# RWKV preparation: the inverse of the cumulative decay by a second scan and one Newton step

## The chip, the cores and the metric

The kernel runs on one core of a Trainium2 chip. The metric is device time in microseconds (us) from start to end of the program; the kernel before takes 1405.99 us (median of three runs, 1405.21 to 1406.52). The engines are named as the profile names them: PE is TensorE's matmul side and PEld its weight load, DVE is VectorE, ACT is ScalarE, POOL is GpSimd, SP is the queue from which most DMAs are issued.

## The reference, cut to what matters

One decoder layer for 1024 tokens and width 1024: a mixing part (HGRN2, windowed attention and RWKV-7 side by side), an MLP with a short convolution, a gated embedding, a final norm. The change lies in the RWKV-7 part, whose reference is a recurrence over the tokens with a per-channel decay:

```python
w = -jax.nn.softplus(-(w0 + jnp.tanh(wd) @ w2)) - 0.5
decay = jnp.exp(-jnp.exp(w))
a = jax.nn.sigmoid(a0 + ad @ a2)
...
def step(state, inp):
    r_t, w_t, k_t, v_t, kk_t, a_t = inp
    sa = jnp.einsum('bhvk,bhk->bhv', state, -kk_t)
    state = (state * w_t[:, :, None, :] + sa[..., None] * (kk_t * a_t)[:, :, None, :]
             + v_t[..., None] * k_t[:, :, None, :])
    return state, jnp.einsum('bhvk,bhk->bhv', state, r_t)
```

The decay of a token equals exp(-e^-0.5 * s), where s is the sigmoid of the decay's low-rank projection. The kernel does not walk through the tokens one by one. It works in chunks of 64 tokens, and for each chunk needs the running product of the decays from the chunk's start (gamma) and its inverse 1/gamma, for each channel and token.

## The kernel before, in words

Everything is held with channels on the 128 partitions and tokens along the free dimension, 1024 of them, in two halves of 512. A projection is a product of a 1024 x 128 block of weights with the normed input; both are split into a high and a low part, and three matmuls (lines 137, 139 and 141) stand in for one. A block's 48 matmuls write a `dp` tile, of which there are two in PSUM. Before that its weights come by DMA (`wraw`, line 105), ACT makes the high part (`whi`, line 114), and POOL or DVE the low part (`wlo`, line 116), in turn.

The RWKV part runs twice, for channel pair p = 0 and p = 1 (each 128 channels, two heads). In each, `rwkv_prep` makes the operands: k by a projection and a mix with the previous token (`mix_in`), the sums of squares of its key (`kks`), the decay `w` and the gate `a` (sigmoids on ACT, lines 568 and 571, from two small matmuls each), then exp (line 572), the scan that gives `gam` (line 581), the reciprocals that give `ig` (line 584, two halves), `ai = a * ig` (586), r by another projection (its `mix_in` scales the `dp` tile in line 320 and reads it a last time in line 502), `kkn`, `bhat` (602), and `ar` (609). A scan over a whole row would run across chunks. So the first column of each chunk is copied into `dz`, which is zero elsewhere, and set to zero in `w`: the step state = w * state + dz then starts anew at each chunk.

`bhat` and `ar` go into 32 small matmuls, the scores (`sc`, line 654 in `rwkv_scores`). They are masked (656), written to DRAM and read back in another layout (`scz`, `At`, lines 664 and 670). `rwkv_inverse` then inverts 32 x 32 blocks on DVE: 31 pairs of a multiply and an add (lines 678 and 680). The result goes through DRAM once more (`Tz`, `Tc`, lines 685 and 690) and `rwkv_join` multiplies with it (`py`, line 790), with which `rwkv_main` begins.

PE has other work in the meantime: `project_rest`, a generator that projects blocks for the later parts. It is called `fill`, and the prep and the inverse draw steps from it.

What sets the order of the work: the code is recorded once, and a scheduler then fixes the order of the instructions of each engine by its own estimates of their durations. At run time each engine and each DMA queue works strictly in that order, and an instruction that waits holds up all that stands behind it on its engine. The scheduler also gives out buffers: the tiles with tag `tr` share eight.

Of the kernel before, what the change touches and what calls it, by code (L numbers as in the profile page):

```python
# [13 lines left out]
AF = mybir.ActivationFunctionType  # L14
ALU = mybir.AluOpType
# [5 lines left out]
HT = 512  # L21
# [4 lines left out]
EXP_M05 = math.exp(-0.5)  # L26
# [4 lines left out]
PC_W0, PC_A0, PC_KK, PC_KA, PC_RK, PC_LNW, PC_LNB = 48, 50, 52, 54, 56, 58, 60  # L31
# [58 lines left out]
class Trunk:  # L90
# [446 lines left out]
    def rwkv_prep(self, p, tp, lt, d, fill):  # L537

        nc, par = self.nc, self.par

        def tr(name):
            return tp.tile([P, T], F32, tag="tr", name=self.nm(name), bufs=8)

        def col(c):
            return par[:, c + p:c + p + 1]

        k = self.mix_in(2 + 3 * p, 2 + p, "k", tr)
        if p == 0:
            self.load_masks(tp)
            self.ps0.close()  # L550
            self.mxp = self.psm.enter_context(self.pool("mx", bufs=4, space=PSUM))
        mxp = self.mxp

        sq = tr("kksq")
        nc.scalar.activation(sq, k, AF.Square, scale=col(PC_KK))
        pss = mxp.tile([P, 16], F32, tag="mx", name=self.nm("kks"))
        for tb in range(8):
            nc.tensor.matmul(pss[:, 2 * tb:2 * tb + 2], sq[:, tb * P:(tb + 1) * P], self.bone2, start=True, stop=True)
        r1 = self.spool.tile([P, 16], F32, tag="kr1", name=self.nm("kr1"), bufs=1)
        nc.vector.tensor_scalar(r1, pss, 1e-24, None, ALU.max)  # L560
        r2 = self.spool.tile([P, 16], F32, tag="kr2", name=self.nm("kr2"), bufs=1)
        nc.gpsimd.tensor_tensor(r2, r1, self.mhalf, ALU.pow)
        w, a = tr("w"), tr("a")
        for hf in (0, 1):
            sl = slice(hf * HT, (hf + 1) * HT)
            ps = mxp.tile([P, HT], F32, tag="mx", name=self.nm("lo"))
            nc.tensor.matmul(ps, par[0:64, PC_LORA + p * P:PC_LORA + (p + 1) * P], lt[0:64, sl], start=True, stop=True)
            nc.scalar.activation(w[:, sl], ps, AF.Sigmoid, bias=col(PC_W0))
            ps = mxp.tile([P, HT], F32, tag="mx", name=self.nm("lo"))
            nc.tensor.matmul(ps, par[64:128, PC_LORA + p * P:PC_LORA + (p + 1) * P], lt[64:128, sl], start=True, stop=True)  # L570
            nc.scalar.activation(a[:, sl], ps, AF.Sigmoid, bias=col(PC_A0))
        nc.scalar.activation(w, w, AF.Exp, scale=-EXP_M05)

        dz = tr("dz")
        w3 = w.rearrange("p (c i) -> p c i", i=64)
        dz3 = dz.rearrange("p (c i) -> p c i", i=64)
        nc.gpsimd.memset(dz, 0.0)
        nc.vector.tensor_copy(dz3[:, :, 0:1], w3[:, :, 0:1])
        nc.vector.memset(w3[:, :, 0:1], 0.0)
        gam = tr("gam")  # L580
        nc.vector.tensor_tensor_scan(gam, w, dz, 0.0, ALU.mult, ALU.add)
        ig = tr("ig")
        for hf in (0, 1):
            nc.vector.reciprocal(ig[:, hf * HT:(hf + 1) * HT], gam[:, hf * HT:(hf + 1) * HT])  # L584
        ai = tr("ai")
        nc.vector.tensor_tensor(ai, a, ig, ALU.mult)
        r = self.mix_in(3 + 3 * p, 0 + p, "r", tr)

        kkn = tr("kkn")
        for hf in (0, 1):  # L590
            sl = slice(hf * HT, (hf + 1) * HT)
            pb = mxp.tile([P, HT], F32, tag="mx", name=self.nm("kkb"))
            self.spread2(pb, r2[:, 8 * hf:8 * hf + 8], 4)
            nc.vector.scalar_tensor_tensor(kkn[:, sl], k[:, sl], self.nkk[:, p:p + 1], pb, ALU.mult, ALU.mult)
        ar = self.slots.tile([P, 2, 16, 64], F32, tag="rk_ar", name=self.nm("ar"), bufs=1)

        def c3(t):
            return t.rearrange("p (c i) -> p c i", i=64)

        g3, kk3 = c3(gam), c3(kkn)  # L600
        be, kh = self.slot("bhat"), self.slot("khat")
        nc.vector.scalar_tensor_tensor(be, ai, -1.0, kkn, ALU.mult, ALU.mult)
        def pairs(t, odd, turn=False):
            t = t.rearrange("p (a b) i -> p a b i", b=4)[:, :, 2 * odd:2 * odd + 2]
            return t[:, :, ::-1] if odd and turn else t

        for odd in (0, 1):
            a4, k4, g4 = pairs(ar[:, 0], odd, True), pairs(kk3, odd), pairs(g3, odd)
            nc.vector.tensor_tensor(a4[:, :, :, 1:], k4[:, :, :, 1:], g4[:, :, :, :63], ALU.mult)
            nc.scalar.copy(a4[:, :, :, 0:1], k4[:, :, :, 0:1])  # L610
        d.update(ar=ar, be=be, kh=kh)
        for _ in range(6 if p else 8):
            next(fill)
        self.rwkv_scores(p, tp, d)
        if p:
            d["v"] = self.mix_in(4 + 3 * p, 4 + p, "v")

        t = tr("ka")
        nc.vector.tensor_scalar(t, a, -1.0, col(PC_KA), ALU.add, ALU.mult)
        nc.vector.scalar_tensor_tensor(k, t, 1.0, k, ALU.add, ALU.mult)  # L620
        for odd in (0, 1):
            nc.vector.tensor_tensor(pairs(ar[:, 1], odd, True), pairs(c3(r), odd), pairs(g3, odd), ALU.mult)
        nc.gpsimd.tensor_tensor(kh, k, ig, ALU.mult)
        gC = self.spool.tile([P, 16], F32, tag="gC", name=self.nm("gC"), bufs=1)
        self.gap = nc.vector.tensor_copy(gC.unsqueeze(2), g3[:, :, 63:64]).ins
        bv = self.slot("bv")
        nc.vector.scalar_tensor_tensor(bv, r, col(PC_RK), k, ALU.mult, ALU.mult)
        d.update(bv=bv, gC=gC)
# [1231 lines left out]
```

## Time and profile before

| | |
|---|---|
| median of three runs | 1405.99 us |
| profiled execution | 1404.77 us |
| its span, first to last instruction | 1403.0 us |
| PE, DVE, ACT, POOL busy | 98%, 76%, 44%, 28% of the span |
| prep of p = 0, and of p = 1 | about 47 to 80 us, and 214 to 242 us |
| two reciprocals of one prep, back to back | 6.55 us (p = 0), 6.57 us (p = 1) |
| one scan | 2.29 us |

A row of the timeline gives the start in us from the span's start, the duration in us, engine, line, operation, the tiles as out<-in, and in brackets the idle time before it and what ended it. A row of the windows gives the stretch, its length, then for PE, PEld, DVE, ACT and POOL the busy time and (in brackets) the number of instructions, and at its end the granted PE clock, the DMA share and GB/s. A row of the waits gives who waited for whom, the total in us, how often, and the longest.

### The profile page before, as it was taken

Reading aid. Unit: us, or ns where it says so; the run is one execution under the profiler, and the core shown is the slowest. Engines: PE = TensorE matmul, PEld = TensorE weight load, DVE = VectorE, ACT = ScalarE, POOL = GpSimd, SP = SyncE. Lnnn points to the kernel's source line nnn. Section 1 sums busy time; section 2 is a strip of 40 time slices with the busy share of each in tenths; the row PEclk is TensorE's granted clock in tenths of the full one; section 3 lists DMA queues with packets and bytes.
Section 4 is the critical chain, followed back from the end, with each engine's and each line's share of the span. In section 5 each row is a group of like instructions: output and inputs, shape, how many; then the busy total and the mean of one; then the engine's idle time right before and its main releaser. Section 6 shows DMA issues by size and latency. Waiting matters only on the chain.

```text
span 1403.0 us, 22344 instructions
## 1 busy us (share of the span) xinstructions
PE 1375.7 (98%) x8644; PEld 1116.5 (80%) x8644; DVE 1063.7 (76%) x1613; ACT 611.8 (44%) x1049; POOL 395.5 (28%) x287
## 2 busy tenths in 40 slices
PE   9999999999999999999999999999999999999997
PEld 6878777877878768788788888888888888888886
DVE  7696456835667796468889888888988799777685
ACT  7522323133255584255544343444344444455542
POOL 5411012101222242221345454545453000002342
PEclk9999999999999999999999999999999999999998
DMA  6123111321622212653232332332324963441443
GB/s 224 61 83 104 64 61 47 100 73 62 225 83 99 91 61 71 253 180 125 94 127 98 113 103 90 102 105 98 114 98 166 351 217 106 127 143 45 136 138 140
DMA packets 80122, 167.61 MB, mean 119 GB/s; under 512 B 19984, under 2 KB 22288, under 8 KB 80016
## 3 DMA queue, kind: packets, MB, share of 16 engines
q1 hardware_dynamic: 66784, 147.05, 31.3%
q10 hardware_dynamic: 12224, 15.47, 3.2%
q0 software_dynamic: 1008, 3.67, 0.7%
q8 instruction: 68, 1.11, 0.3%
q14 instruction: 38, 0.31, 0.1%
HBM read 119.76 MB, written 46.40 MB: 118 GB/s over the span
## 4 chain that ended last, share of the span: by engine, by line
PE 78%; DVE 8%; issue 8%; ACT 3%; POOL 3%; DMA 1%; SPq 0%; POOLq 0%; ACTq 0%; DVEq 0%
PE bg L1338 17%; PE bv L1338 13%; PE bv L1639 7%; PE bg L1639 7%; PE dp L137 7%; PE dp L139 7%; PE dp L141 7%; PE swq L1169 1%; DVE ig L584 1%; PE hsc L1015 1%; PE zp L137 1%; DVE xl L409 1%; PE zp L141 1%; PE zp L139 1%; PE swo L1209 1%
## 5 line engine op out<-in xcount | busy, mean ns | idle before, releaser
L137 PE MATMUL dp<-xh,whi 128*128 128x512 f32 x544 | 186.9, 406 | 1.2 <-DVE r L502 0.7
L139 PE MATMUL dp<-xl,whi 128*128 128x512 f32 x544 | 180.5, 394 | 0.6 <-DVE xl L409 0.5
L141 PE MATMUL dp<-xh,wlo 128*128 128x512 f32 x544 | 179.7, 392 | 0.0
L116 POOL TENSOR_TENSOR wlo<-wraw,whi 128x512 fp32r<-128x512 f32 x60 | 84.5, 1410 | 264.9 <-ACT whi L114 226.8
L116 POOL TENSOR_TENSOR wlo<-raw,whi 128x512 fp32r<-128x512 f32 x84 | 135.0, 1626 | 75.9 <-ACT whi L114 75.9
L114 ACT CAST whi<-wraw 128x512 fp32r<-128x512 f32 x120 | 72.9, 618 | 158.0 <-PE dp L139 103.0
L1338 PE MATMUL bg<-t,whi 128*128 128x512 f32 x352 | 133.4, 389 | 0.0
L139 PEld LDWEIGHTS dp<-xl,whi 128*128 128x128 f32 x544 | 102.3, 188 | 24.6 <-DVE xl L409 2.5
L141 PEld LDWEIGHTS dp<-xh,wlo 128*128 128x128 f32 x544 | 102.2, 188 | 23.8 <-issue 2.0
L137 PEld LDWEIGHTS dp<-xh,whi 128*128 128x128 f32 x544 | 98.8, 189 | 26.0 <-issue 3.9
L116 POOL TENSOR_TENSOR wlo<-s,whi 128x512 fp32r<-128x512 f32 x44 | 64.5, 1466 | 168.6 <-ACT whi L114 168.6
L1639 PE MATMUL bg<-t,whi 128*128 128x512 f32 x308 | 95.2, 390 | 0.0
L1639 PE MATMUL bv<-t,whi 128*128 128x512 f32 x308 | 94.8, 389 | 0.0
L114 ACT CAST whi<-raw 128x512 fp32r<-128x512 f32 x88 | 52.7, 620 | 93.7 <-issue 48.5
L114 ACT CAST whi<-s 128x512 fp32r<-128x512 f32 x66 | 38.9, 620 | 120.2 <-PE bg L1338 112.8
L1338 PEld LDWEIGHTS bg<-t,whi 128*128 128x128 f32 x352 | 66.1, 188 | 13.7
L190 POOL TENSOR_TENSOR rst<-rst,mhalf 128x4 f32<-128x4 f32 (+1 forms) x9 | 10.2, 1134 | 234.0 <-DVE rst L186 218.0
L1635 ACT CAST t<-t 128x512 fp32r<-128x512 f32 x77 | 47.8, 622 | 45.8 <-PE bv L1639 32.7
L1338 PE MATMUL bg<-t,wlo 128*128 128x512 f32 x176 | 67.5, 389 | 0.0
L1639 PEld LDWEIGHTS bv<-t,whi 128*128 128x128 f32 x308 | 57.8, 188 | 12.0
L1639 PEld LDWEIGHTS bg<-t,whi 128*128 128x128 f32 x308 | 57.8, 188 | 11.9
L116 DVE TENSOR_TENSOR wlo<-wraw,whi 128x512 fp32r<-128x512 f32 x60 | 48.2, 807 | 20.7 <-ACT whi L114 18.5
(417 smaller groups left out, 3423.6 us busy)
## 6 DMA issues: line engine op xcount, KB each, us to landing
raw<-in_ffn_up_dram SPq DMA_DIRECT2D x44, 512.0 KB, 3.5
wraw<-in_w_in_dram SPq DMA_DIRECT2D x28, 512.0 KB, 3.4
z<-zst SPq DMA_DIRECT2D x18, 512.0 KB, 2.9
gb<-ct SPq DMA_DIRECT2D x33, 256.0 KB, 2.3
t<-gb SPq DMA_DIRECT2D x33, 256.0 KB, 2.7
t<-gt SPq DMA_DIRECT2D x33, 256.0 KB, 2.7
zl<-z SPq DMA_DIRECT2D x16, 512.0 KB, 4.4
wraw<-in_ple_gate_dram SPq DMA_DIRECT2D x16, 512.0 KB, 3.4
```

The costliest lines, as they stand in the source:

```text
L114: self.cast = nc.scalar.copy(hi, src).ins
L116: eng.tensor_tensor(lo, src, hi.bitcast(F32), ALU.subtract)
L137: nc.tensor.matmul(ps[hf], wh, xh[hf], start=first, stop=False)
L139: nc.tensor.matmul(ps[hf], wh, xl[hf], start=False, stop=False)
L141: self.step = nc.tensor.matmul(ps[hf], wl, xh[hf], start=False, stop=last).ins
L409: nc.vector.scalar_tensor_tensor(lo, x, g[:, k:k + 1], hi.bitcast(F32), ALU.mult, ALU.subtract)
L584: nc.vector.reciprocal(ig[:, hf * HT:(hf + 1) * HT], gam[:, hf * HT:(hf + 1) * HT])
L1015: nc.tensor.matmul(sc[g:g + 64, c, :], ks[:, c * P + g:c * P + g + 64], x, start=True, stop=True)
L1169: m = nc.tensor.matmul(pq[h][:, b:b + w], d["q"][hs, qb * P:nk], d["k"][hs, b:b + w], start=True, stop=True)
L1338: nc.tensor.matmul(ps, w[part == 2][:, s], X[k][part == 1], start=start and k == part == 0, stop=k == 3 and part == 2, skip_group_check=no ...
L1635: nc.scalar.copy(xh, x)
L1639: nc.tensor.matmul(ps[m], wt[part == 2][:, m * P:(m + 1) * P], (xh, xl)[part == 1], start=k == part == 0, stop=k == NK - 1 and part == 2)
```

## The change: what it does, and the diff

ACT computes a second exponential, exp(+e^-0.5 * s), the inverse of a token's decay, into the tile `gam`, ahead of the exponential of the decay itself. For p = 1 the last sigmoid of `a` is fixed behind both exponentials. DVE then scans twice: the running product of the inverses goes into `ig`, then that of the decays into `gam`. Two fused steps take the place of the reciprocals, and do one Newton step on `ig`: w = -gam * ig, then ig = (w + 2) * ig. So per prep there are one activation, one scan, two fused steps of 128 x 1024, one copy and one memset of 128 x 16 more, and two reciprocals of 128 x 512 less. No DMA and no matmul is added or removed.

```diff
-            nc.scalar.activation(a[:, sl], ps, AF.Sigmoid, bias=col(PC_A0))
-        nc.scalar.activation(w, w, AF.Exp, scale=-EXP_M05)
+            if not (p and hf):
+                nc.scalar.activation(a[:, sl], ps, AF.Sigmoid, bias=col(PC_A0))
+        gam = tr("gam")
+        nc.scalar.activation(gam, w, AF.Exp, scale=EXP_M05)
+        m = nc.scalar.activation(w, w, AF.Exp, scale=-EXP_M05)
+        if p:
+            with self.tc.issue_after(m.ins):
+                nc.scalar.activation(a[:, sl], ps, AF.Sigmoid, bias=col(PC_A0))
 
         dz = tr("dz")
-        w3 = w.rearrange("p (c i) -> p c i", i=64)
         dz3 = dz.rearrange("p (c i) -> p c i", i=64)
         nc.gpsimd.memset(dz, 0.0)
-        nc.vector.tensor_copy(dz3[:, :, 0:1], w3[:, :, 0:1])
-        nc.vector.memset(w3[:, :, 0:1], 0.0)
-        gam = tr("gam")
-        nc.vector.tensor_tensor_scan(gam, w, dz, 0.0, ALU.mult, ALU.add)
         ig = tr("ig")
-        for hf in (0, 1):
-            nc.vector.reciprocal(ig[:, hf * HT:(hf + 1) * HT], gam[:, hf * HT:(hf + 1) * HT])
+        for src, dst in ((gam, ig), (w, gam)):
+            s3 = src.rearrange("p (c i) -> p c i", i=64)
+            nc.vector.tensor_copy(dz3[:, :, 0:1], s3[:, :, 0:1])
+            nc.vector.memset(s3[:, :, 0:1], 0.0)
+            nc.vector.tensor_tensor_scan(dst, src, dz, 0.0, ALU.mult, ALU.add)
+        nc.vector.scalar_tensor_tensor(w, gam, -1.0, ig, ALU.mult, ALU.mult)
+        nc.vector.scalar_tensor_tensor(ig, w, 2.0, ig, ALU.add, ALU.mult)
         ai = tr("ai")
```

In the changed file the new scan is line 588, the fused steps are 589 and 590, and what stands behind them has a line number 6 higher than before (the scores are line 660).

The change also moves instructions that it does not name, because the scheduler orders them anew. On PE, in p = 0, before (`dp_619` is one block of `fill`, `dp_827` the next):

```order
L141 MATMUL dp_619<-xh_119,wlo_617 128x512
L141 MATMUL dp_619<-xh_103,wlo_617 128x512
L137 MATMUL dp_827<-xh_105,whi_646 128x512
L137 MATMUL dp_827<-xh_89,whi_646 128x512
L139 MATMUL dp_827<-xl_106,whi_646 128x512
L139 MATMUL dp_827<-xl_90,whi_646 128x512
L141 MATMUL dp_827<-xh_105,wlo_648 128x512
L141 MATMUL dp_827<-xh_89,wlo_648 128x512
L137 MATMUL dp_827<-xh_107,whi_646 128x512
L137 MATMUL dp_827<-xh_91,whi_646 128x512
L139 MATMUL dp_827<-xl_108,whi_646 128x512
L654 MATMUL sc_679<-ar_601,bhat_602 64x64
```

and of the change (the same two blocks are `dp_623` and `dp_831`):

```order
L141 MATMUL dp_623<-xh_119,wlo_621 128x512
L141 MATMUL dp_623<-xh_103,wlo_621 128x512
L660 MATMUL sc_683<-ar_605,bhat_606 64x64
L660 MATMUL sc_684<-ar_605,bhat_606 64x64
L660 MATMUL sc_683<-ar_605,bhat_606 64x64
```

The scores now stand straight behind the first block; the nine matmuls of the next block that stood ahead of them come after all 32 of them.

On PE, in p = 1, before (`dp_2263` is a block of `fill`, `dp_2361` the projection of v):

```order
L141 MATMUL dp_2263<-xh_99,wlo_2261 128x512
L137 MATMUL dp_2361<-xh_105,whi_2353 128x512
L137 MATMUL dp_2361<-xh_89,whi_2353 128x512
L139 MATMUL dp_2361<-xl_106,whi_2353 128x512
L139 MATMUL dp_2361<-xl_90,whi_2353 128x512
L141 MATMUL dp_2361<-xh_105,wlo_2355 128x512
L141 MATMUL dp_2361<-xh_89,wlo_2355 128x512
L137 MATMUL dp_2361<-xh_107,whi_2353 128x512
L137 MATMUL dp_2361<-xh_91,whi_2353 128x512
L139 MATMUL dp_2361<-xl_108,whi_2353 128x512
L139 MATMUL dp_2361<-xl_92,whi_2353 128x512
L654 MATMUL sc_2311<-ar_2245,bhat_2246 64x64
```

and of the change (`dp_2263` is `dp_2271` there):

```order
L141 MATMUL dp_2271<-xh_99,wlo_2269 128x512
L660 MATMUL sc_2319<-ar_2253,bhat_2254 64x64
L660 MATMUL sc_2320<-ar_2253,bhat_2254 64x64
L660 MATMUL sc_2319<-ar_2253,bhat_2254 64x64
L660 MATMUL sc_2320<-ar_2253,bhat_2254 64x64
```

Here ten matmuls of the projection of v, among them the one that had to wait for a free `dp` tile, are moved behind the scores.

On POOL, in p = 1, before (`khat` is line 623, `Tb` the memsets ahead of the inverse):

```order
L116 TENSOR_TENSOR wlo_2359<-wraw_2351,whi_2357 128x512
L116 TENSOR_TENSOR wlo_2564<-wraw_2556,whi_2562 128x512
L672 MEMSET Tb_2431 64x1024
L673 MEMSET Tb_2431 64x32
L623 TENSOR_TENSOR khat_2247<-k_2117,ig_2156 128x1024
L116 TENSOR_TENSOR wlo_2629<-wraw_2625,whi_2627 128x512
```

and of the change:

```order
L116 TENSOR_TENSOR wlo_2367<-wraw_2359,whi_2365 128x512
L678 MEMSET Tb_2439 64x1024
L679 MEMSET Tb_2439 64x32
L116 TENSOR_TENSOR wlo_2572<-wraw_2564,whi_2570 128x512
L116 TENSOR_TENSOR wlo_2637<-wraw_2633,whi_2635 128x512
L629 TENSOR_TENSOR khat_2255<-k_2121,ig_2158 128x1024
```

`khat` now comes behind a second `wlo`. On DVE the new steps stand in the order of the code, with r's scaling (line 320) ahead of the second scan's copy in p = 0 and between the two fused steps in p = 1; the small copy `gC` comes ahead of `ai` in both. On SP the weight load that stood on one side of the reads of `At` stands on the other: in p = 0 it is now ahead of them, in p = 1 behind them.

## The prediction, made before the changed kernel ran

> **What bounds the kernel now.** I read first the page's shares, then the windows around the two places that the change touches, then PE's waits there.
>
> ```profile
> span 1403.0 us, 22344 instructions
> PE 1375.7 (98%) x8644; PEld 1116.5 (80%) x8644; DVE 1063.7 (76%) x1613; ACT 611.8 (44%) x1049; POOL 395.5 (28%) x287
> ```
> ```profile
> 47.00:80.00 33.00, 32.03 (x230) 25.54 (x229) 26.30 (x29) 16.09 (x21) 9.55 (x5) 1.00 0.10 33
> 80.00:132.00 52.00, 52.00 (x227) 42.36 (x226) 41.83 (x84) 11.20 (x16) 8.77 (x8) 1.00 0.37 107
> 214.00:242.00 28.00, 26.61 (x204) 20.57 (x203) 20.72 (x23) 9.93 (x14) 5.07 (x3) 1.00 0.06 20
> 242.00:290.00 48.00, 48.00 (x209) 38.73 (x207) 36.66 (x79) 5.88 (x9) 9.79 (x8) 1.00 0.35 108
> ```
> PE is the bound: in the preps (first and third row) it is busy 32.03 of 33 and 26.61 of 28 us, and behind each it has no hole at all (52.00 of 52.00, 48.00 of 48.00). Its clock is 1.00 in all four. So a faster DVE is worth only what PE waits for it in the preps:
>
> ```profile
> PE sc L654 <- DVE ar L609: 1.4, 2, 0.8
> PE dp L137 <- DVE r L502: 0.7, 1, 0.7
> ```
> That is 2.1 us in the whole program (the scores of both preps, and once a `dp` tile that r's last read frees). It is the ceiling on what this change can win. What it can lose is not bounded by it, since PE's order changes as well.
>
> **DVE's part: what the new steps cost.** For p = 0:
>
> ```profile
> 60.44 0.19 DVE L578 COPY dz<-w 128x16 f32<-128x16 f32 x1 [5.18 <-ACT w L572]
> 60.81 2.29 DVE L581 TENSOR_TENSOR_SCAN gam<-w,dz 128x1024 f32<-128x1024 f32 x1
> 63.02 1.21 DVE L320 TENSOR_TENSOR dp<-dp,rstd 128x1024 f32<-128x1024 f32 x1
> 64.14 6.55 DVE L584 RECIPROCAL ig<-gam 128x512 f32<-128x512 f32 x2
> 70.73 1.23 DVE L586 TENSOR_TENSOR ai<-a,ig 128x1024 f32<-128x1024 f32 x1
> 75.04 1.22 DVE L602 SCALAR_TENSOR_TENSOR bhat<-ai,kkn 128x1024 f32<-128x1024 f32 x1
> ```
> From the start of the reciprocals to `ai`: 70.73 - 64.14 = 6.59 us. In their place stand a copy and memset (start to start of the scan 60.81 - 60.44 = 0.37), a scan (2.29), and two fused steps. These have two SBUF operands of 128 x 1024, as `bhat` has, so 1.22 each. Sum 0.37 + 2.29 + 2.44 = 5.10, with some 0.15 for `gC`'s place and for steps that each need the one before: 5.25. DVE gains 6.59 - 5.25 = 1.3 us. ACT's new exponential lies under the first scan: that scan needs the first exponential alone, and starts when it did.
>
> For p = 1:
>
> ```profile
> 222.37 2.29 DVE L581 TENSOR_TENSOR_SCAN gam<-w,dz 128x1024 f32<-128x1024 f32 x1
> 224.70 6.57 DVE L584 RECIPROCAL ig<-gam 128x512 f32<-128x512 f32 x2
> 231.18 1.21 DVE L320 TENSOR_TENSOR dp<-dp,rstd 128x1024 f32<-128x1024 f32 x1
> 232.29 1.21 DVE L586 TENSOR_TENSOR ai<-a,ig 128x1024 f32<-128x1024 f32 x1
> ```
> The reciprocals take 231.18 - 224.70 = 6.48 on the path, the new steps 5.2: again 1.3. The chain from `ai` to `ar` is the same in both versions, so the scores are ready 1.3 us earlier, if nothing else holds the new steps up.
>
> **What holds them up: POOL.**
>
> ```profile
> 61.46 2.74 POOL L116 TENSOR_TENSOR wlo<-wraw,whi 128x512 fp32r<-128x512 f32 x1 [2.54 <-ACT whi L114]
> 69.01 1.30 POOL L116 TENSOR_TENSOR wlo<-wraw,whi 128x512 fp32r<-128x512 f32 x1 [4.81 <-ACT whi L114]
> 89.56 1.30 POOL L116 TENSOR_TENSOR wlo<-wraw,whi 128x512 fp32r<-128x512 f32 x1 [7.39 <-ACT whi L114]
> ```
> ```profile
> 89.61 1.29 DVE L678 TENSOR_TENSOR Tt<-At,Tb 64x31 f32<-64x31 f32 x1
> 253.70 0.17 DVE L678 TENSOR_TENSOR Tt<-At,Tb 64x31 f32<-64x31 f32 x1
> ```
> A multiply that takes 0.17 us took 1.29 when POOL's `wlo` began just before it (89.56): it stood still for 1.1 us, until POOL was done (90.86). The other way round, the `wlo` of 61.46 met the running scan, and took 2.74: it ended 1.1 us after the scan's end (63.10). But the `wlo` of 69.01 ran its usual 1.30 beside the reciprocals, and those took no longer. So a reciprocal and a `wlo` pass each other, a two-operand step and a `wlo` exclude each other, and the one that asked first goes first. The change replaces the former kind by the latter. In p = 0 the second fused step runs from about 64.14 + 0.37 + 2.29 + 1.22 = 68.0 to 69.3, so POOL's `wlo`, ready at 69.01, waits for it and then goes ahead of `ai`: `ai` loses about 1.1. For p = 1:
>
> ```profile
> 220.84 1.06 ACT L572 ACTIVATE w<-w 128x1024 f32<-128x1024 f32 x1
> 224.02 0.62 ACT L114 CAST whi<-wraw 128x512 fp32r<-128x512 f32 x1
> ```
> The cast that stood at 224.02 comes 1.06 later, behind the new exponential, and ends at 225.7; its `wlo` then meets the second scan (about 225.0 to 227.3), waits for its end, and goes ahead of the first fused step: 1.1 lost again. So of DVE's gain g = 1.3 there is left 0.2 in each prep. The bounds of g are 0.2 (hit) and 1.3 (missed); I take 0.2, since the hit in p = 1 has a window of 2.3 us, and that in p = 0 one of about 1.2.
>
> The Trainium skill, SBUF — State Buffer, section "SBUF: two separate sides", states this as a lock: DVE with two SBUF inputs and a GpSimd operation that reads SBUF share one pair of ports, the first has it for its whole instruction, the other is blocked. The rows above agree with it, and by it the sum is the one with g = 0.2; without it, that with g = 1.3.
>
> **PE's part: the scores are moved forward.** PE's rows in p = 0:
>
> ```profile
> 73.73 0.39 PE L141 MATMUL dp<-xh,wlo 128*128 128x512 f32 x1
> 75.78 0.39 PE L139 MATMUL dp<-xl,whi 128*128 128x512 f32 x1
> 77.00 1.52 PE L654 MATMUL sc<-ar,bhat 64*64 64x64 f32 x64 [0.83 <-DVE ar L609]
> ```
> Before, PE ended its last matmul ahead of the scores at 75.78 + 0.39 = 76.17, and stood for 0.83 until 77.00. Now the nine matmuls from 73.96 on stand behind the scores. PE comes to them at 73.73 + 0.39 = 74.12 and stands until 77.00 - g, so 2.88 - g. The nine are done later, but nothing fills the hole. The loss is 2.88 - g - 0.83 = 2.05 - g: 1.85 us with g = 0.2, 0.75 with 1.3. And in p = 1:
>
> ```profile
> 234.10 0.61 PE L141 MATMUL dp<-xh,wlo 128*128 128x512 f32 x2
> 235.41 0.72 PE L137 MATMUL dp<-xh,whi 128*128 128x512 f32 x2 [0.70 <-DVE r L502]
> 237.37 0.63 PE L139 MATMUL dp<-xl,whi 128*128 128x512 f32 x2
> 238.55 1.52 PE L654 MATMUL sc<-ar,bhat 64*64 64x64 f32 x64 [0.56 <-DVE ar L609]
> ```
> Before: a wait of 0.70 for the tile and 0.56 for `ar`, together 1.26. Now PE is free at 234.10 + 0.61 = 234.71 and stands until 238.55 - g, so 3.84 - g; the tile is free by then. Loss 2.58 - g: 2.38 with g = 0.2, 1.28 with 1.3. Since PE has no hole behind, every later matmul moves by as much.
>
> **POOL's `khat`, and the inverse.** Behind the scores of p = 1, `khat` moves from a stretch in which DVE waits to one where it works:
>
> ```profile
> 246.06 2.39 POOL L623 TENSOR_TENSOR khat<-k,ig 128x1024 f32<-128x1024 f32 x1
> 251.91 1.27 POOL L116 TENSOR_TENSOR wlo<-wraw,whi 128x512 fp32r<-128x512 f32 x1 [3.46 <-ACT whi L114]
> ```
> ```profile
> 250.09 1.28 DVE L627 SCALAR_TENSOR_TENSOR bv<-r,par,k 128x1024 f32<-128x1024 f32 x1
> ```
> ```profile
> 290.32 0.24 PE L790 MATMUL py<-Tc,sc 32*32 32x32 f32 x2
> 290.96 1.19 PE L790 MATMUL py<-Tc,sc 32*32 32x32 f32 x62
> PEld py L790 <- DMA Tc<-Tz: 0.8, 2, 0.5
> ```
> It follows the second `wlo`, the one that stood at 251.91 and whose cast now comes ahead of v's step on ACT, so it falls on `bv` (250.09) or on the first multiplies of the inverse, all with two operands. It costs that chain between 0 (it falls beside steps that read PSUM) and 2.4 (its whole length); I take 1.0, near the 1.1 of a usual block. The chain ends in `Tc`, and there is no slack: `py` started as its weights came (the last row), PE stood between its two pieces, and so 1.0 goes to PE. In p = 0 `khat` keeps its place. There a `wlo` of DVE (0.7) moves into the inverse, and the weight load goes ahead of `At` on SP; the reads of `Tc` are issued long before `py` there:
>
> ```profile
> 125.55 2.18 SPq L690 DMA_DIRECT2D Tc<-Tz  x4
> ```
> until 127.73, and PE has work until about 132.8. I cost these at nothing; cover gone, they would cost about 0.7. ACT's later casts (by 1.06) feed blocks that PE reaches many us later: nothing.
>
> **Sum.** 1.85 + 2.38 + 1.0 = 5.2 us. The profiled execution took 1404.77 (span 1403.0), so 1410.0; the median of the runs is 1.2 above it, 1405.99, so 1411.2.
>
> **Rivals.** *No collision:* POOL misses the new steps, g = 1.3, and `khat` costs nothing: 0.75 + 1.28 = 2.0, time 1408.0. For it: POOL's starts depend on tenths of a us. With one or two of the three hits, 3.1 to 4.2 are lost (1409.1 to 1410.2). *Not slower:* the fused steps are cheaper than `bhat`'s row, and the scheduler was right to move the scores. The point where this decides is g = 2.05 in p = 0 and 2.58 in p = 1; each fused step would need (6.59 - 2.05 - 2.81) / 2 = 0.87, or (6.48 - 2.58 - 2.81) / 2 = 0.55 us, where 2.81 is the rest of the 5.25. At that point the time is 1406.0, and at the ceiling of 2.1 us won 1403.9. Against it: 1.22 in two places for this shape. *More collisions:* `khat` costs its full 2.4, and p = 0's inverse comes late by 0.7: 1.85 + 2.38 + 2.4 + 0.7 = 7.3, time 1413.3.
>
> **How the numbers follow.** Forecast (all three costs) 0.45; one or two of the three 0.13; no collision 0.14; not slower 0.10; more collisions 0.12; something else 0.06. A measurement of this kernel can tell 0.2%, 2.8 us, from no change. Slower: 0.45 + 0.13 + 0.12 = 0.70. Within 0.2%: 0.14 and nearly all of "not slower", 0.23. Faster: 0.07, all but from what I don't see, since even the ceiling of 2.1 us does not reach it. The range leaves out "not slower" and a little on top: 1406.5 to 1413.8.
>
> **What will show it.** Right: PE's wait at the scores is 2.5 to 2.8 us in p = 0 and 3.5 to 3.8 in p = 1 and the one for r's tile is gone; `ai` (p = 0) and the first fused step (p = 1) last about 2.3 us beside a `wlo`; the fused steps otherwise last 1.22; `py` of p = 1 waits 1 us longer. Wrong: waits at the scores under 1 us, which would mean cheaper steps, or later stretches in which PE wins back what it lost.

## The result, and the profile after

The kernel after the change takes 1414.65 us (median of six runs, 1412.75 to 1415.97), the kernel before 1405.7 us beside it. The ratio is 1.0065, with a 95% interval of 1.0054 to 1.0076: slower by some 9 us, where 5.2 were forecast. The direction was right, and the size falls just outside the range (1413.8).

The page of the profiled execution, which took 1412.75 us:

```profile
span 1411.0 us, 22350 instructions
PE 1377.6 (98%) x8644; PEld 1119.1 (79%) x8644; DVE 1063.7 (75%) x1619; ACT 613.4 (43%) x1051; POOL 397.2 (28%) x287
```

The span is 8.0 us longer than before (1403.0). PE's busy time grew by 1.9 us, though it runs the same 8644 matmuls; the other 6.1 us are waits. The windows around the two preps, as shown of the kernel before:

```profile
47.00:80.00 33.00, 30.29 (x222) 24.10 (x221) 25.92 (x30) 17.86 (x23) 8.80 (x5) 1.00 0.09 33
80.00:132.00 52.00, 52.00 (x227) 42.36 (x226) 40.66 (x85) 9.77 (x15) 8.50 (x7) 1.00 0.37 103
214.00:242.00 28.00, 24.33 (x165) 19.05 (x167) 19.28 (x22) 12.00 (x16) 7.84 (x5) 0.96 0.11 38
242.00:290.00 48.00, 47.88 (x237) 38.60 (x230) 36.00 (x73) 5.98 (x9) 9.75 (x6) 0.95 0.28 94
```

In the preps (first and third row) PE is busy 1.74 and 2.28 us less than before. What is new stands near the end of the rows, in the column of the granted clock: 0.96 and 0.95 around 242 us, where it was 1.00. PE's waits in whole:

```profile
PE sc L660 <- DVE ar L615: 6.3, 3, 3.6
PE py L796 <- DMA Tc<-Tz: 0.6, 1, 0.6
```

The wait at the scores is 6.3 us (2.46 and 0.25 for p = 0, 3.56 for p = 1), where there were 1.4 before; the wait of 0.7 us for r's `dp` tile is gone; at `py` of p = 1 PE stands for 0.57 us between its two pieces, where it stood for 0.40 before (290.96 - 290.32 - 0.24). PE's rows at the scores, first p = 0, then p = 1:

```profile
77.33 0.34 PE L660 MATMUL sc<-ar,bhat 64*64 64x64 f32 x8 [2.46 <-DVE ar L615]
77.92 1.04 PE L660 MATMUL sc<-ar,bhat 64*64 64x64 f32 x56 [0.25 <-DVE ar L615]
...
240.72 2.36 PE L660 MATMUL sc<-ar,bhat 64*64 64x64 f32 x64 [3.56 <-DVE ar L615]
243.02 1.22 PE L137 MATMUL dp<-xh,whi 128*128 128x512 f32 x2
...
246.59 0.71 PE L139 MATMUL dp<-xl,whi 128*128 128x512 f32 x2
247.14 0.62 PE L141 MATMUL dp<-xh,wlo 128*128 128x512 f32 x2
247.60 0.62 PE L137 MATMUL dp<-xh,whi 128*128 128x512 f32 x2
```

Behind the hole of p = 1 the same work takes longer. The 64 small matmuls of the scores last 2.36 us instead of 1.52. The eight large matmuls from 243.02 on need 3.57 us (246.59 - 243.02), where eight at the pace of the last two rows (two in 247.60 - 247.14 = 0.46) need 1.84. Together PE loses 0.84 + 1.73 = 2.6 us there. The windows of 2 us show why:

```profile
238.00:240.00 2.00, 0.00 (x0) 0.00 (x0) 2.00 (x4) 0.31 (x2) 0.00 (x0) 0.98 0.00 0
240.00:242.00 2.00, 1.17 (x33) 1.04 (x37) 2.00 (x3) 0.00 (x0) 1.09 (x2) 0.50 0.00 0
242.00:244.00 2.00, 2.00 (x45) 1.73 (x38) 2.00 (x6) 0.00 (x0) 0.00 (x0) 0.50 0.03 8
244.00:246.00 2.00, 2.00 (x6) 1.57 (x5) 1.49 (x3) 0.00 (x0) 0.00 (x0) 0.50 0.44 178
246.00:248.00 2.00, 2.00 (x8) 1.60 (x8) 0.00 (x0) 0.00 (x0) 0.00 (x0) 0.81 0.21 85
```

The clock is granted at half from about 239.9 to 246.8 us, that is from near the end of a hole of 3.56 us in which PE did nothing. Behind the hole of 2.46 us in p = 0 it stayed at 1.00 in this execution (second row of the first windows).

So the 8.0 us are, by rows: 1.88 more of waiting at the scores of p = 0 (2.46 + 0.25 - 0.83), 2.30 at those of p = 1 (3.56 - 1.26), and 2.6 of half clock; 1.2 are left. Of these, 0.7 us stand ahead of the first prep already, where DVE's first new step starts at 61.18 us, its counterpart before at 60.44. The rest falls far behind the preps: the same matmuls run 7.4 us later than before at 500 us and 8.1 us later at 527 us, on either side of the wait for `vt`.

DVE's rows, p = 0 and p = 1, and then the two rows of POOL that fall on them:

```profile
67.57 1.23 DVE L589 SCALAR_TENSOR_TENSOR w<-gam,ig 128x1024 f32<-128x1024 f32 x1
...
70.09 2.20 DVE L592 TENSOR_TENSOR ai<-a,ig 128x1024 f32<-128x1024 f32 x1
...
229.95 2.13 DVE L589 SCALAR_TENSOR_TENSOR w<-gam,ig 128x1024 f32<-128x1024 f32 x1
233.14 1.21 DVE L590 SCALAR_TENSOR_TENSOR ig<-w,ig 128x1024 f32<-128x1024 f32 x1
```
```profile
69.76 1.45 POOL L116 TENSOR_TENSOR wlo<-wraw,whi 128x512 fp32r<-128x512 f32 x1 [4.83 <-ACT whi L114]
...
228.05 2.95 POOL L116 TENSOR_TENSOR wlo<-wraw,whi 128x512 fp32r<-128x512 f32 x1 [4.83 <-ACT whi L114]
```

A fused step takes 1.21 to 1.23 us, as forecast. `ai` takes 2.20 behind the `wlo` of 69.76, and the first fused step of p = 1 takes 2.13 behind the `wlo` of 228.05, which had waited for the end of the scan: both collisions, in the places named.

### The profile page after: what moved, and what is told of

It reads as the page before. It is cut to its first block, busy times and chain, and to the rows that moved or that the text cites. A ratio compares the mean times of both kernels' runs of the same rounds, so it can differ in the third digit from the quotient of the medians.

```text
span 1411.0 us, 22350 instructions
## 1 busy us (share of the span) xinstructions
PE 1377.6 (98%) x8644; PEld 1119.1 (79%) x8644; DVE 1063.7 (75%) x1619; ACT 613.4 (43%) x1051; POOL 397.2 (28%) x287
## 4 chain that ended last, share of the span: by engine, by line
PE 77%; DVE 8%; issue 8%; ACT 3%; POOL 2%; DMA 1%; SPq 0%; POOLq 0%; ACTq 0%; DVEq 0%
PE bg L1344 17%; PE bv L1344 13%; PE bv L1645 7%; PE bg L1645 7%; PE dp L137 7%; PE dp L139 7%; PE dp L141 7%; PE hsc L1021 1%; PE zp L137 1%; PE swq L1175 1%; DVE xl L409 1%; PE swo L1215 1%; PE zp L141 1%; PE zp L139 1%; PE swt L1201 1%
```

## The experiments

The theory after this comparison, called "order and clock": the loss comes from PE's order (the scores ahead of 9 and 10 matmuls), by the waits in front of the scores and by the half clock that such a wait brings. Its rivals: the waits alone; the new arithmetic and its collisions; something behind the preps (`khat`, the inverse, moved transfers).

**e1: the order alone, with the reciprocals.** The kernel before, in which the matmuls that the scores had behind them in the change are tied behind the last of the scores:

```diff
+                    self.lastsc = nc.tensor.matmul(ps[h][col, m, :], be3[row, t, :], ..., start=True, stop=True).ins
...
+            with self.tc.issue_after(self.lastsc):
+                d["v"] = self.mix_in(4 + 3 * p, 4 + p, "v")
...
+                with tc.issue_after(self.lastsc):
+                    next(fill)
```

> The kernel before, with its reciprocals, but PE's order of the change: the scores of both preps ahead of the 9 and the 10 matmuls. Theory (order and clock): PE stands 0.83 + 2.05 = 2.9 us at the scores of p = 0 and 0.56 + 0.70 + 2.58 = 3.8 us at those of p = 1; behind the longer hole the granted clock is 0.50 for some 7 us, which costs 2.2. Sum 2.05 + 2.58 + 2.2 = 6.8 us over the kernel before (1412.5); 9 if the hole of 2.9 drops the clock too. Rival (waits alone): 4.6 us over the kernel before, clock 1.00 behind both holes. Rival (the new arithmetic costs the time: scan, fused steps, collisions with POOL): no more than 1 us over the kernel before.

Measured: 1416.11 us, the kernel before 1405.2 beside it, ratio 1.0074 (1.0061 to 1.0087). The order alone is at least as slow as the change (1.0065). PE's rows at the scores, and the windows behind them:

```profile
77.59 2.15 PE L657 MATMUL sc<-ar,bhat 64*64 64x64 f32 x64 [2.89 <-DVE ar L611]
...
244.24 2.15 PE L657 MATMUL sc<-ar,bhat 64*64 64x64 f32 x64 [3.83 <-DVE ar L611]
```
```profile
76.00:78.00 2.00, 0.41 (x16) 0.44 (x16) 2.00 (x4) 0.00 (x0) 0.00 (x0) 0.84 0.00 0
78.00:80.00 2.00, 2.00 (x61) 1.83 (x54) 2.00 (x5) 0.00 (x0) 0.74 (x1) 0.50 0.03 8
80.00:82.00 2.00, 2.00 (x8) 1.59 (x8) 2.00 (x3) 0.00 (x0) 2.00 (x2) 0.80 0.31 125
...
244.00:246.00 2.00, 1.62 (x60) 1.55 (x64) 2.00 (x4) 0.00 (x0) 0.66 (x2) 0.66 0.00 0
```

The holes are those that the prediction worked out for g = 0 (2.88 and 3.84), and the clock halves behind both. The rival that blames the arithmetic is out. The loss of 10.9 us is also more than the 6.8 or 9 of the theory, so its sum was short as well. In the profiled execution, 13.0 us longer than that of the kernel before, two more stretches of half clock are what it lacked: one behind a wait of 1.93 us at `yt` (the clock is 0.50 from 204 to 206 us), one behind waits of 0.72 and 0.67 us at `py` of p = 1 (0.50 from 304 to 306 us), with 1.7 us of clock each.

**e2: no Newton step.** Lines 589 and 590 are left out (with the ties of e1, to hold PE's order).

```diff
-        nc.vector.scalar_tensor_tensor(w, gam, -1.0, ig, ALU.mult, ALU.mult)
-        nc.vector.scalar_tensor_tensor(ig, w, 2.0, ig, ALU.add, ALU.mult)
```

> The change without its two fused steps (the inverse is left as the second scan gives it, so the refinement is not computed), PE's order kept. DVE reaches ar 2.4 us earlier from the steps, and up to 1.1 more in each prep where the collision with POOL's wlo falls away. Theory (order and clock): no hole over 0.3 us at the scores of p = 0, 0.2 to 1.2 at those of p = 1, clock 1.00 behind both, so 2.5 + 2.4 to 3.4 + 2.2 = 7.1 to 8.1 us less than the change: 1406.5 to 1407.5. Rival (waits alone, no clock): 4.9 to 5.9 less, 1408.7 to 1409.7.

Measured: 1411.15 us, ratio 1.0041 (1.0028 to 1.0054). A miss for both, and not for their reason: the scheduler moved v's projection of p = 0 forward, into the middle of a filling block, and PE stood behind the scores instead of ahead of them:

```profile
84.11 1.22 PE L137 MATMUL dp<-xh,whi 128*128 128x512 f32 x2 [5.09 <-ACT zst L457]
```

It waits for a `dp` tile, which ACT had not yet read out. This run tells nothing of the holes at the scores; e8 repeats it without this one.

**e3: work that nothing uses, in the hole of p = 1.**

```diff
             ps = [mxp.tile([P, 4, 64], F32, tag="mx", name=self.nm("sc")) for _ in (0, 1)]
+            if p and g == 0:
+                with self.tc.issue_after(self.step):
+                    for _ in range(4):
+                        nc.tensor.matmul(ps[0].rearrange("p m i -> p (m i)"), self.ident, d["k"][:, 0:256], start=True, stop=True)
```

> The change with four matmuls of 128 x 256 that nothing uses, put into the hole ahead of the scores of p = 1 (they write the tile that the scores then overwrite). DVE's chain and the moment at which the scores start stay. Theory (the hole drops the clock): the hole is cut to less than 2.5 us without work, the granted clock stays 1.00 behind it, the scores take 1.52 instead of 2.36 us, and the kernel is 2.2 us shorter than the change although PE does more. Rival (the clock drops for another reason, or its drop costs nothing on the path): the same time as the change, within 0.5 us.

Measured: 1413.36 us, ratio 1.0065 (1.0051 to 1.0079), the profiled execution 1412.1. The windows around the hole of p = 1, and those of p = 0 of the same execution:

```profile
76.00:78.00 2.00, 0.82 (x33) 0.75 (x37) 2.00 (x4) 0.00 (x0) 0.00 (x0) 0.94 0.00 0
78.00:80.00 2.00, 2.00 (x45) 1.77 (x38) 2.00 (x5) 0.00 (x0) 1.41 (x1) 0.50 0.03 8
80.00:82.00 2.00, 2.00 (x8) 1.55 (x7) 2.00 (x4) 0.00 (x0) 2.00 (x2) 0.71 0.35 145
238.00:244.00 6.00, 3.92 (x77) 3.09 (x76) 6.00 (x9) 0.31 (x2) 1.10 (x2) 1.00 0.01 3
244.00:252.00 8.00, 8.00 (x37) 6.62 (x36) 2.56 (x6) 0.62 (x1) 1.04 (x1) 1.00 0.38 98
```

Where PE had something to do in the hole, the clock stayed at 1.00 behind it, though DVE, the scores' start and all else stayed as they were: the hole is the cause of the drop. But the time did not come down by 2.2 us, nor by anything that can be measured (the change's ratio is 1.0065); and in this execution the clock did drop in p = 0, behind a hole of 2.46 us, as long as the one that left it alone above. And what was won at the scores of p = 1 was lost at `py`: PE waited there for 1.32 us in one piece, and the clock dropped behind it, by (0.02 + 0.15) x 10 = 1.7 us between 290 and 310 us:

```profile
300.00:310.00 10.00, 10.00 (x150) 7.26 (x150) 1.15 (x4) 5.03 (x12) 0.00 (x0) 0.85 0.13 54
```

**e4: two more filling steps ahead of the scores, in both preps.**

```diff
-        for _ in range(6 if p else 8):
+        for _ in range(8 if p else 10):
             next(fill)
```

(The loop behind the inverse draws as many fewer, and asks for v's projection of p = 0 at `i == 0` instead of `i == 1`.)

> The change, with two more steps of the filling projection (12 matmuls) drawn ahead of the scores in each prep. Theory (order and clock): 12 matmuls take 2.7 us, so the holes of 2.5 and 3.6 us shrink to under 0.3 and 0.9, the clock stays 1.00, and 2.3 + 2.7 + 2.2 = 7.2 us come back: 1405.6 to 1407.4, the time of the kernel before. Rival (the loss lies in later stretches, as khat, the inverse or the moved transfers): the holes go but the time stays over 1410.

Measured: 1411.97 us, ratio 1.0049 (1.0036 to 1.0063). The hole at the scores of p = 0 went, but as in e2 v's projection came into the middle of a filling block, and its wait took the place:

```profile
84.59 1.22 PE L137 MATMUL dp<-xh,whi 128*128 128x512 f32 x2 [3.85 <-ACT zst L457]
```

A hole that is only moved wins little or nothing: the interval overlaps that of the change (1.0054 to 1.0076).

**e5: the change once more.**

> The change itself once more, for a second profile beside the others of this group. Theory (order and clock, the clock set by what share of a window of some 3.4 us PE stands): the holes at the scores are 2.5 and 3.6 us again; the clock drops behind the second in every execution, and behind the first in some and not in others, so that executions of this one kernel differ by 1 to 2 us and the median stays near 1414.6. Rival (waits alone): the executions differ by no more than those of the kernel before.

Measured: 1413.47 us (1412.39 to 1415.25), ratio 1.0058 (1.0045 to 1.0071). The profiled execution took 1415.09. Its windows of p = 0 and p = 1:

```profile
78.00:80.00 2.00, 2.00 (x57) 1.79 (x58) 2.00 (x4) 0.00 (x0) 0.95 (x1) 0.59 0.04 8
80.00:82.00 2.00, 2.00 (x7) 1.55 (x6) 2.00 (x4) 0.00 (x0) 2.00 (x2) 0.56 0.13 53
...
242.00:244.00 2.00, 1.56 (x48) 1.43 (x52) 2.00 (x4) 0.00 (x0) 0.75 (x2) 0.55 0.04 8
```

The same program, with the same holes (2.47 and 3.56 us), this time with half clock behind both; it ran 2.3 us longer than the execution profiled first. Behind p = 0 PE lost (1.00 - 0.59) x 2 + (1.00 - 0.56) x 2 = 1.7 us of clock. The kernel before, too, varied by 2.3 us over its 21 runs beside this group (1404.42 to 1406.76), so the spread of the times alone does not speak for the theory; the two profiles do.

**e6: work that nothing uses, in both holes.** As e3, with three such matmuls for p = 0, and v's projection of p = 0 asked for at `i == 7`.

> The change with matmuls that nothing uses in both holes ahead of the scores: 3 of 128 x 256 for p = 0, 4 for p = 1 (they write the tile that the scores then overwrite; v's projection of p = 0 is asked for six steps later, so that PE's order behind the scores stays). The scores start no earlier than in the change. Theory (order and clock): the waits stay (1.65 + 2.3 us against the kernel before), the clock is 1.00 behind both, so 4.0 to 4.5 us over the kernel before: 1409.2 to 1410.2, 4 to 5 under the change. Rival (the clock matters in p = 1 alone): 2.2 under the change, 1412 to 1412.5.

Measured: 1413.07 us (1411.31 to 1414.2), ratio 1.0053 (1.0039 to 1.0067); a miss. In the profiled execution, which took 1411.31, the clock is 1.00 in both preps, as meant. But `py` of p = 1 waits more than twice as long as in the change:

```profile
296.90 1.19 PE L800 MATMUL py<-Tc,sc 32*32 32x32 f32 x62 [1.44 <-DMA Tc<-Tz]
```

PE, no longer slowed, comes to `py` before the inverse is there. Part of what the clock gives is taken back by this wait. The profiled execution is the fastest of the five, and the only one with a mean granted clock of 0.994; the other four have 0.992 to 0.993, that is some 3 to 6 us more of half clock in 1410. So the idle matmuls did not keep the clock in each execution; in which place it dropped in the others, no profile shows.

**e7: the matmuls put back ahead of the scores, and v's projection behind the whole filling block.** As e4, and:

```diff
-                if p == 0 and i == 1:
+                if p == 0 and i == 5:
                     d["v"] = self.mix_in(4, 4, "v")
```

> The change with 12 matmuls of the filling projection ahead of the scores in each prep, as in the fourth experiment, but v's projection of p = 0 is asked for behind the whole of the second filling tile, as PE ran them before. Theory (order and clock): the hole of 3.9 us behind the scores of p = 0 goes; PE stands about 0.2 us at the scores of p = 0, 1.2 at those of p = 1 and 1.4 at py, against 0.8, 1.3 and 0.6 before, clock 1.00: 1404.8 to 1406.5, the same as the kernel before within 0.1%. Rival (the new arithmetic or its collisions cost time elsewhere): over 1408.

Measured: 1405.02 us, ratio 0.9994 (0.9985 to 1.0003): the time of the kernel before, with the new arithmetic in place, and 8.4 us under the change in the same group (1413.47). PE's rows:

```profile
77.90 1.44 PE L660 MATMUL sc<-ar,bhat 64*64 64x64 f32 x64
...
238.68 0.34 PE L660 MATMUL sc<-ar,bhat 64*64 64x64 f32 x8 [1.20 <-DVE ar L615]
...
291.43 0.24 PE L796 MATMUL py<-Tc,sc 32*32 32x32 f32 x2 [1.50 <-DMA Tc<-Tz]
```

So, with operands as late as the change has them, the whole loss lies in where the scores stand in PE's order. The wait of 1.50 at `py` is the one that e6 showed.

**e8: e2 with the order held.** Lines 589 and 590 left out, v's projection of p = 0 asked for at `i == 7`, and that of p = 1 tied behind the last of the scores.

> The change without its two fused steps (the refinement of the inverse is left out), as in the second experiment, but with v's projection of p = 0 behind the whole filling tile, so that PE's order is that of the change. Theory (order and clock): the hole of 5.1 us behind the scores of p = 0 goes, PE stands 0.2 at the scores of p = 0, 0.5 at those of p = 1, 0.8 at py, clock 1.00: 1404.2 to 1405.6, 9 to 10 us under the change for two steps of 1.2 us in each prep. Rival (waits alone; the loss of the second experiment was not that hole): 1409 to 1411.

Measured: 1403.67 us, ratio 0.9987 (0.9978 to 0.9995), 0.5 us under the forecast. With DVE's chain 2.4 us shorter (and without the collision on `ai`), PE's order of the change is no harm: 9.8 us under it. What the scores ahead of the filling block cost depends on how late their operands are.

**e9: e4's edit for p = 1 alone.**

```diff
-        for _ in range(6 if p else 8):
+        for _ in range(8):
             next(fill)
```

> The change with the 12 matmuls of the filling projection ahead of the scores of p = 1 alone; p = 0 is left as in the change. Theory (order and clock): of the 8.5 us between the change (1413.5) and the seventh experiment (1405.0), p = 0 keeps its wait of 2.2 us and, in some executions, a clock drop of up to 1.7: 1407.2 to 1408.9. So p = 1 gives back 4.6 to 6.3. Rival (waits alone): p = 1 gives back its 2.4 us of waiting, 1411.

Measured: 1407.58 us, ratio 1.0014 (1.0005 to 1.0023), as the theory had it. So p = 1 gives back 5.9 us of the 8.4 (1413.47 - 1407.58), and p = 0 the other 2.6 (1407.58 - 1405.02); by the ratios, each against the kernel before beside it, 6.2 and 2.8. In the profiled executions the waits at the scores of p = 1 fell from 3.56 to 1.06 us, so 2.5; that the rest is half clock and what follows from it is argued, not measured by this run.

**e10: `bv` and `khat` out of the inverse's way.** As e7, and in `rwkv_prep`:

```diff
-        if p:
-            d["v"] = self.mix_in(4 + 3 * p, 4 + p, "v")
...
         d.update(bv=bv, gC=gC)
+        if p:
+            d["v"] = self.mix_in(4 + 3 * p, 4 + p, "v")
```

> The seventh experiment, with v's projection of p = 1 asked for behind bv, so that bv (DVE, 1.3 us) and khat (POOL) run in the stretch in which DVE has nothing, instead of behind the scaling of v's tile and ahead of the first multiply of the inverse. One wlo passes from POOL to DVE ahead of ai (0.7 us, against the 1.1 us of the collision that it takes away). Theory (the inverse of p = 1 starts late, since DVE's queue holds bv and meets khat): its first multiply comes 1.3 to 2.4 us earlier, the wait of 1.5 us at py falls under 0.5, 1403.0 to 1404.5. Rival (py waits for something else, as the transfers): py still waits 1.5 us, 1404.6 to 1405.5.

Measured: 1403.31 us, ratio 0.9984 (0.9975 to 0.9993): faster than both kernels. First the rows of e7 at the start of the inverse of p = 1 (DVE, then POOL), then DVE's and PE's of e10:

```profile
252.63 1.40 DVE L633 SCALAR_TENSOR_TENSOR bv<-r,par,k 128x1024 f32<-128x1024 f32 x1
255.15 1.19 DVE L684 TENSOR_TENSOR Tt<-At,Tb 64x31 f32<-64x31 f32 x1
```
```profile
252.90 3.39 POOL L629 TENSOR_TENSOR khat<-k,ig 128x1024 f32<-128x1024 f32 x1
```
```profile
252.45 0.18 DVE L683 TENSOR_TENSOR Tt<-At,Tb 64x31 f32<-64x31 f32 x1
```
```profile
237.83 0.34 PE L659 MATMUL sc<-ar,bhat 64*64 64x64 f32 x8 [0.40 <-ACT whi L114]
238.42 1.04 PE L659 MATMUL sc<-ar,bhat 64*64 64x64 f32 x56 [0.25 <-DVE ar L615]
288.99 0.24 PE L795 MATMUL py<-Tc,sc 32*32 32x32 f32 x2
```

In e7 `khat` falls on the first multiply, which takes 1.19 instead of 0.18 us, and `bv` stands ahead of it; in e10 the multiply starts 2.7 us earlier, and `py` starts without a wait. 0.85 us of that come from the scores, which start earlier (238.68 and 237.83) and wait 0.65 us instead of 1.45.

**e11: the reciprocals in the order of e10.** The kernel before with the edits of e7 and e10.

> The kernel before, with its reciprocals, and the edits of the tenth experiment (12 filling matmuls ahead of the scores, v of p = 0 behind the filling tile, v of p = 1 behind bv). Theory (the new arithmetic gains 0.2 to 1.3 us in each prep, PE's order is the rest): 0 to 2 us over the tenth experiment, 1403.5 to 1405.5. Rival (the new arithmetic itself costs time): faster than the tenth experiment by more than 1 us.

Measured: 1405.03 us, ratio 1.0000 (0.9991 to 1.0009). In the same order, the change's arithmetic is worth 1.7 us (1405.03 - 1403.31; the two intervals overlap a little).

**e12: e8 with the edit of e10.**

> The eighth experiment (no fused steps: the refinement of the inverse is left out; 8 and 6 filling steps as in the change) with v's projection of p = 1 asked for behind bv. Theory: the two waits of 0.7 us at py of p = 1 go, the waits at the scores stay under 0.6: 1401.5 to 1403.0. Rival (nothing is left to win, since PE has work anyway): 1403.3 to 1404.0, as the eighth.

Measured: 1403.17 us, ratio 0.9986 (0.9977 to 0.9995), between the two forecasts. Its ratio is all but that of e8 (0.9987), so it gains nothing that these runs can tell.

**e13 and e14: with the wait at `py` away, is the half clock seen in the time?** e13 is e6, and e14 the change, both with v of p = 1 asked for behind `bv` as in e10, and v of p = 0 at `i == 7`.

> The sixth experiment (idle matmuls in both holes ahead of the scores) with v's projection of p = 1 asked for behind bv, so that the wait at py falls away as in the tenth. Theory (order and clock): the waits at the scores are left, 1.65 us more than the kernel before for p = 0 and 1.8 to 2.3 more for p = 1, and nothing else: 1408.8 to 1410.2. Rival (the clock costs the median nothing; the rest is lost elsewhere): 1412 to 1413, as the sixth.

> The change with v's projection of p = 1 asked for behind bv, and no idle matmuls: the holes at the scores stay at about 2.5 and 3.1 us (the collision of the first fused step with POOL gives way to a wlo of 0.7 on DVE). Theory (order and clock): the clock drops behind the hole of p = 1 and in some executions behind that of p = 0, so PE comes to py late anyway and the missing wait wins little: 1411.8 to 1414, 2.5 to 4.5 over the thirteenth. Rival (the clock costs the median nothing): within 1 us of the thirteenth.

Measured: 1411.02 us (ratio 1.0036, 1.0024 to 1.0049) and 1411.15 us (1.0036, 1.0023 to 1.0050). By the times the rival holds: no difference. The profile of e13 shows where the clock went:

```profile
290.00:300.00 10.00, 8.99 (x97) 7.43 (x96) 1.81 (x3) 2.70 (x5) 0.00 (x0) 0.89 0.59 105
300.00:310.00 10.00, 10.00 (x166) 7.13 (x169) 1.15 (x4) 4.10 (x10) 0.00 (x0) 0.94 0.14 56
```

In e13 the clock is 1.00 at the scores, but PE then waits at `py` for 1.0 us all the same, and the clock drops there, by (0.11 + 0.06) x 10 = 1.7 us of clock. In e14 it drops behind both scores, and once more behind a wait of 1.93 us at `yt` (0.50 from 206 to 208 us), and PE comes to `py` without a wait. So the half clock at the scores and the wait (with its own half clock) at `py` stand in for each other. Either way 7 to 8 us (1411.0 and 1411.2 against the 1403.3 of e10; 7.3 by the ratios) are lost through the position of the scores; how many of them are "clock" is not a fixed number.

## Why the prediction was right or wrong

- **PE bounds the kernel, and DVE's speed can win 2.1 us at most: nothing speaks against it.** In an order that suits both, the arithmetic is worth 1.7 us (e10 against e11).
- **The price of the new steps: right.** A scan of 2.29 and two steps of 1.22 were forecast; 2.29 and 1.21 to 1.23 were measured. From the second copy (64.88) to `ai` (70.09) pass 5.21 us in p = 0; 5.25 was the sum.
- **The collisions with POOL: right in both places**, `ai` in p = 0 and the first fused step in p = 1, with 0.97 and 0.9 us lost, where 1.1 were put. The Trainium skill, SBUF — State Buffer, section "SBUF: two separate sides", states it as a lock, by which one of the two is blocked until the other ends; the rows agree.
- **The waits at the scores: right.** Forecast 2.5 to 2.8 and 3.5 to 3.8 us, measured 2.71 (in two pieces) and 3.56; the loss by them 1.88 and 2.30, where 1.85 and 2.38 stood in the sum.
- **`khat` and the inverse, 1.0 us at `py`: the collision came, the wait didn't.** `bv` took 1.52 us and the first multiply 1.15 instead of 0.17. But PE stands at `py` for 0.57 us, 0.17 more than before, because it comes there late by itself. The first multiply stands on DVE behind the scaling of v's tile, which waits for v's projection (10.46 us in the change, 5.60 before); ten matmuls of that projection had moved behind the scores and ran at half clock, so PE and the inverse came late together. Once PE is kept at full clock it waits 1.44 us (e6), and 1.50 where its work is put back (e7): the size was about right, but the prediction's "there is no slack" no longer held.
- **The step that failed: PE's part.** It took a hole for the price of its length ("The loss is 2.88 - g - 0.83"). It left out that PE's clock drops behind such holes (and stays, in e3 and e6, where idle matmuls fill them). The sum lacks a term of 2.6 us behind the scores of p = 1 in one profiled execution, and of 1.7 more behind those of p = 0 in the other. It also holds the 1.0 us of `khat`, which did not come at PE; without it the sum would have been 4.2 us, so that the forecast is no more than 3.5 us off (1414.65 - 1411.2) is in part luck. The kernel before already showed the kind of thing, in a place that I did not weigh: at 508.8 us PE waits 2.4 us for `vt` (line 1049), and the window behind it has a clock of 0.66.

```profile
510.00:515.00 5.00, 3.79 (x37) 3.21 (x38) 4.19 (x8) 4.71 (x7) 3.49 (x3) 0.66 0.41 120
```

The windows that the prediction read for the clock were those around the preps, in which there was no such hole yet.

- **The rivals.** "Not slower" is out, "no collision" too. "More collisions" named 1413.3, nearest to the time, but for another reason: none of its extra costs (the 2.4 of `khat`, a late inverse in p = 0) shows at PE.
- **What stays open.** The idle matmuls of e3 and e6 kept the clock in p = 1, and in both preps, in the profiled executions, but moved the median by nothing that can be measured, and e13 and e14 are level. The profiles show two things that take its place (the wait at `py`, and in e3 and e13 a drop behind it). How the 9 us of the medians divide into waits and half clock is therefore not shown; only profiled executions can be divided.

## What to carry to other kernels

A scheduler's new order is part of a change: where the bounding engine's filling work slips behind an instruction that waits, the wait and all that hangs on it are lost, and drawing the same work ahead of it again (e7) took 8.4 us back without touching the arithmetic. In these runs a hole on PE of 2 to 4 us cost its length and, where half clock followed, some 1.7 to 2.6 us more; so look behind the holes that are there already for what the clock did. Before crediting the removal of a stall, ask which later wait it uncovers: here the half clock and the wait at `py` replaced each other.

## What the runs showed of the hardware

The half clock lasts for one or two equal stretches. From the windows (a share of 0.59 in 2 us is 0.41 x 2 / 0.5 = 1.64 us at half) it lasted 1.64 + 1.76 = 3.40 us behind p = 0 in e5, 0.64 + 2 + 0.80 = 3.44 in e1, 0.24 + 2 + 1.16 = 3.40 in e3, and 0.08 + 2 + 2 + 2 + 0.76 = 6.84 behind p = 1 in the change. The Trainium skill, TensorE: Matmul & The Clock Gate, section "What's actually happening", says that a free-running window of 3413 ns decides on the clock; these lengths are one and two of them. The starts agree as well: in e1 the clock halves at 77.36 and at 244.64 us, 167.28 us apart, which is 49.0 such windows.

A hole of 2.46 to 2.47 us in one place, p = 0 of the change and of its variants, left the clock alone in the first profile and in e9, and halved it in e3, e5 and e14. Stretches of 3.41 us, laid end to end from a start of half clock in the same profile, show why. These are the windows of the two that the hole touches in the change, and then of the one that it touches in e5:

```profile
72.68:76.09 3.41, 2.19 (x10) 1.50 (x8) 3.41 (x5) 0.83 (x3) 0.00 (x0) 1.00 0.00 0
76.09:79.51 3.42, 1.93 (x67) 1.70 (x68) 3.42 (x6) 0.00 (x0) 0.52 (x1) 1.00 0.02 5
```
```profile
74.95:78.36 3.41, 0.72 (x33) 0.65 (x37) 3.41 (x5) 0.77 (x3) 0.00 (x0) 1.00 0.00 0
```

In the change the hole lies across a boundary, and PE is idle for 1.22 us of one stretch and 1.49 of the next; in e5 one stretch holds all of it, and PE is idle for 2.69 us. Counted in this way over all sixteen profiles, from 20 us on and without the program's end, 22 stretches at full clock have 1.86 us of idle PE or more, and half clock follows each of them. Of those with 1.85 us or less it follows three, all of them at `py`, among small matmuls (1.39 us in e1, 1.42 in e3, 1.01 in e13); others at `py` with as much (1.46 in e9, 1.50 in e7) were not followed by it, and these runs do not show why.

The Trainium skill, TensorE: Matmul & The Clock Gate, section "Why this matters for your kernels", advises against gaps of over some 3 us; here 2.46 us were enough, and in e1 and e14 1.93 us. The measurement decides: what a hole shorter than the window costs depends on how much of it falls into one window.
